# Six gate projections moved from direct to seven-product form, the heads' work dealt to three lanes, and a new tile order, in a one-core decoder block

## The chip, the core and the metric

The kernel runs on one core of a Trainium2 chip. Its engines are TensorE (PE, matmuls; PEld is its weight load), VectorE (DVE), ScalarE (ACT), GpSimd (POOL) and SyncE (SP), whose queue issues most DMAs; each works through its own queue of instructions in order. The metric is the device time of one execution in microseconds (us). Where a time is compared, it is the median of several executions.

## The reference

A decoder block on 1024 positions of width 1024 with 16 meta positions in front, one layer, all in float32:

```python
p     = h @ w_in + b_in        # columns: u_s5 | q | k | v | o | i | f | g_s5 | g_m
y_s5  = GLU(GELU(S5(u_s5)))                       # grouped complex-diagonal state-space model
y_m   = (o * HeadNorm(mLSTM(q, k, v, i, f))) @ m_w_out   # 4 heads, chunkwise
mix   = sigmoid(g_s5) * y_s5 + sigmoid(g_m) * y_m
h     = LN(alpha * h + mix @ w_o)
h     = LN(alpha * h + relu(h @ w_up + b_up)^2 @ w_down)
```

Here `o` is a sigmoid of its own projection, and q and k pass through a causal convolution of width 4 and a SiLU.

## The kernel before

Every float32 operand is split into a high and a low part (`whi`, `wlo`; `hT_hi`, `hT_lo`), and every product is made of three matmuls, high by high, low by high and high by low (`mm3`, lines 229 to 237). Features are tiled by 128, positions by up to 512. A projection tile is a **job**: it loads its weights (`wraw`), has them split by ScalarE and VectorE (`split_w`, line 208; the split of the next job is issued while this one runs), and runs 24 matmuls for each block of positions into a PSUM bank, which an engine then evacuates.

The job letters of `ORDER` (line 41) are: q0 to q3 the query and key tiles of a head, v the values, u the input of the state-space part (S5), o the output gates of the mLSTM, g the gates g_s5, m two of the gates g_m. Behind them follow the eight GLU tiles z0 to z7. A gate job has two halves of 512 positions, so 48 matmuls of 128x512.

Everything that is not a projection runs in **lanes** (line 90): generators that issue a few instructions and then yield a number, an estimated time until their next step. `pump()` (line 154), called after every two blocks of a projection, lets each lane go on whose number is used up. So the numbers at the top of the file (`ML`, `NL`, `C5`, `K5`, ...) set how the small instructions are spread among the projections; a list scheduler then fixes the order on each engine. Lane `ml` holds the four heads one behind the other. Head h (`mlstm`, line 438) makes its decay tables (`gB`, `wiB`, `qi`), then goes through nine chunks: per chunk `pk` (transpose of k) and `pS` (scores), then `pn` (read-out with the state `C`) and `pu` (the update). The normalisation `N` (line 503), once for chunks 1 to 4 and once for 5 to 8, ends in the transposes `pt` of `hraw` and two ScalarE evacuations into `hmF`.

An o job multiplies its sigmoid (`osig`) into `hmF`, and needs the head finished. The loop at line 1523 sees to that:

```python
            while int(j.tag[1:]) not in HMREADY:
                lanes["cv"].drain()
                lanes["ml"].step()
```

It issues the steps of the head at once, before the o job's own instructions.

`ah_scale` (line 1405) scales the normed input by alpha times gain and adds alpha times bias, in eight tiles `ahr` of 128x1024 that are loaded from `ah0_dr`, worked on by two VectorE instructions each and stored to `ah_dr`. It starts with o6 and shares lane `ah` with `up_early`, which prepares the first weights of the up projection.

Behind z7 `run7` works through two stages of class `Seven` (line 1024). There a pair of output tiles is computed from quarter blocks by **seven** products in place of eight, with sums of weight blocks that GpSimd's queue has made by accumulating DMAs into `ws_dr` (`w_sums`, line 973), and differences of position blocks that VectorE makes and splits in place into `hT` (`to_home`). A product is a unit of 12 matmuls of 128x512. Stage g has three pairs, the six gates g_m that are not in `ORDER`; stage y has four, the projection `m_w_out`. The units go product by product over all pairs (`SEQ7`). The output projection with its layer norm and the up and down projections follow; these too use seven products.

PSUM has eight banks: five for tag `mm`, three for tag `sd`. SBUF has a pool of 30 slots of 128x1056.

Of the kernel before, what the change touches and what calls it, by code (L numbers as in the profile page):

```python
# [14 lines left out]
P = 128  # L15
# [44 lines left out]
GY = 6.0  # L60
GS = 1.8
# [58 lines left out]
def decoder_block(  # L120
# [7 lines left out]
    big = ctx.enter_context(tc.tile_pool(name="big", bufs=30, side="left"))  # L128
# [22 lines left out]
    lanes = {"ml": Lane(), "cv": Lane(), "s5": Lane(), "s5c": Lane(), "s5g": Lane(), "ah": Lane(), "gp": Lane()}  # L151
# [136 lines left out]
    def qk_job(h, isk):  # L288
# [12 lines left out]
        def conv_steps(pre):  # L301
            y = slot("cy")
            a_.activation(y[:, :LEN], pre[:, 0:LEN], AF.Identity, scale=convt[:, ci, 0:1], bias=convt[:, ci, 4:5])
            for w in range(1, 4):
# [8 lines left out]
            QK[h, isk] = r
            yield 0.5
        fm_job(JQ + ci, BLK0 if len(all_jobs) < 4 else BLK, 0, evac, done)

    def v_job(h):
# [6 lines left out]
        def run(job):  # L324
# [41 lines left out]
            if h == 0:  # L366
                lanes["ml"].add(gates())
# [70 lines left out]
    def mlstm(h):  # L438
        while (h, 1) not in QK:
            yield 0.5  # L440
        qT, kT, vt = QK[h, 0], QK[h, 1], VT[h]
# [15 lines left out]
        yield 4.0
# [45 lines left out]
        def N(half, hm):  # L503
# [12 lines left out]
            for f in range(2):  # L516
# [70 lines left out]
    def s5_pre():  # L587
# [38 lines left out]
        es = slot("s5E")  # L626
        E = es[:, 0:288].rearrange("p (r e q) -> p r e q", r=2, q=16)
# [45 lines left out]
        bb = slot("s5bb")  # L673
        S5["bb"] = bb
# [250 lines left out]
    def glu_job(f):  # L925
        def run(job):
# [6 lines left out]
            MIX[f] = SG.pop(f)  # L933
# [16 lines left out]
            for zz in (1, 0):  # L950
                for bi, (c0, c1) in enumerate(HALF):
# [6 lines left out]
                    else:  # L958
                        v_.tensor_tensor(z2[:, c0:c1], ps, z2[:, c0:c1], op=OP.mult)
# [132 lines left out]
    def gate_evac(n, p, ps):  # L1092
        f1, f2 = NM + 2 * p, NM + 2 * p + 1
# [69 lines left out]
    def gates_and_output():  # L1163
        h00, h10, h01, h11 = home(0, 0), home(1, 0), home(0, 1), home(1, 1)
        g = Seven(3, wf, JGM + NM, 0, {1: h00, 2: h10, 6: h01, 7: h00, 4: h10, 5: h01, 3: h11})
        y = Seven(4, wmo, 0, 3, {1: h00, 2: h10, 6: h01, 7: h11, 4: h00, 5: h10, 3: h01})
# [24 lines left out]
        def hm_load():  # L1191
            for nm, kh, ch in (("11", 0, 0), ("12", 0, 1), ("22", 1, 1), ("21", 1, 0)):
                M[nm] = raw_block(hm_dr, kh, ch)

        def y_start():
            for i in range(3):
# [5 lines left out]
                  7: [lambda: to_home(M["11"], h00), lambda: now(sub(M["12"], M["12"], M["22"]))],  # L1202
# [26 lines left out]
    def ln0_pipe(xs, jobs):  # L1229
# [66 lines left out]
        def pair_banks(p):  # L1296
            tr[p] = [sdps("ln0"), sdps("ln0"), sdps("ln0"), mmps("ln0")]
# [211 lines left out]
    for i, j in enumerate(jobs):  # L1509
# [30 lines left out]
        if i >= 5 and i % 2 and ws:  # L1540
# [583 lines left out]
```

## Time and profile before

| | us |
|---|---|
| median of three executions | 1530.55 |
| lowest and highest of them | 1529.15 and 1532.7 |
| the profiled execution | 1528.6 |
| its span, first to last instruction | 1526.7 |

Times in the profile count from the span's start. The opening layer norm with the first q jobs lasts to about 75 us, the projections with all lanes to 575, the GLU tiles to 664, stage g to 715, stage y to about 790, the output projection with its layer norm to 895, and the up and down projections take the rest. The rows to read are the busy time of each engine by stretch, the waits of TensorE, and the instructions in order of time where it waits. A matmul's row lasts longer than the distance to the next one, since matmuls overlap.

### The profile page before, as it was taken

The numbers are of one execution on the slowest core, as the hardware profiler recorded it, in microseconds if no ns is written. First come the engines' busy times: TensorE is split into PE (matmuls) and PEld (weight loads), VectorE is DVE, ScalarE is ACT, GpSimd is POOL, SyncE is SP. The second block draws the span as 40 slices with busy tenths as digits, with TensorE's granted clock in tenths as the row PEclk, the third lists the DMA queues.
The fourth block names the chain that finished last, engine by engine and source line by source line (L and its number), as shares of the span: only waits on it lengthen the run. The fifth ranks groups of instructions, "written<-read, shape, count | busy, mean of one in ns | idle before, by whom it ended". The sixth has DMA issues, their size and how long they took to land.

```text
span 1526.7 us, 20426 instructions
## 1 busy us (share of the span) xinstructions
PE 1500.7 (98%) x7593; PEld 1269.9 (83%) x7593; DVE 1044.7 (68%) x1895; ACT 659.7 (43%) x1027; POOL 79.9 (5%) x183
## 2 busy tenths in 40 slices
PE   7999899999999998999999999999999999999997
PEld 7998799988998887888788888888888888888886
DVE  7785755447655558768697575766666679767786
ACT  5631644354464453345443253444444534433340
POOL 0000000022032000000000001000000000000000
PEclk9999999999999999999999999999999999999999
DMA  8504132422654369955351238544443897767652
GB/s 304 190 25 137 35 78 80 132 79 89 182 118 97 92 209 350 343 196 191 117 201 70 96 115 265 186 155 149 152 147 134 280 386 274 250 224 237 204 176 100
DMA packets 122147, 261.18 MB, mean 171 GB/s; under 512 B 14568, under 2 KB 36784, under 8 KB 122048
## 3 DMA queue, kind: packets, MB, share of 16 engines
q1 hardware_dynamic: 111344, 233.00, 44.7%
q0 software_dynamic: 10704, 26.88, 7.1%
q8 instruction: 60, 0.98, 0.3%
q14 instruction: 39, 0.32, 0.1%
HBM read 188.78 MB, written 84.55 MB: 179 GB/s over the span
## 4 chain that ended last, share of the span: by engine, by line
PE 78%; issue 16%; DMA 2%; DVE 2%; ACT 1%; SPq 0%; POOLq 0%; ACTq 0%; DVEq 0%
PE mm L235 19%; PE mm L233 19%; PE mm L234 19%; PE sd L234 4%; PE sd L233 4%; PE sd L235 4%; PE mm L1341 2%; DMA x<-in_x_dram 1%; PE pu L483 1%; PE pn L479 1%; PE pn L480 1%; DMA ahr<-ah_dr 1%; DVE ahr L1422 1%; PE pS L469 1%; PE s5z L820 0%
## 5 line engine op out<-in xcount | busy, mean ns | idle before, releaser
L233 PE MATMUL mm<-hT_hi,whi 128*128 128x512 f32 (+3 forms) x604 | 230.2, 381 | 0.0
L235 PE MATMUL mm<-hT_hi,wlo 128*128 128x512 f32 (+3 forms) x604 | 226.3, 377 | 0.1
L234 PE MATMUL mm<-hT_lo,whi 128*128 128x512 f32 (+3 forms) x604 | 225.1, 373 | 0.0
L233 PEld LDWEIGHTS mm<-hT_hi,whi 128*128 128x128 f32 x604 | 113.6, 188 | 18.7 <-issue 1.2
L235 PEld LDWEIGHTS mm<-hT_hi,wlo 128*128 128x128 f32 x604 | 113.5, 188 | 18.4 <-DVE wlo L1063 0.5
L234 PEld LDWEIGHTS mm<-hT_lo,whi 128*128 128x128 f32 x604 | 113.7, 188 | 16.5
L1819 ACT ACTIVATE dah<-da 128x1024 fp32r<-128x1024 f32 x56 | 58.6, 1052 | 89.6 <-PE sd L234 39.6
L234 PE MATMUL sd<-dwl,dah 128*128 128x512 f32 x240 | 94.5, 394 | 0.0
L233 PE MATMUL sd<-dwh,dah 128*128 128x512 f32 x240 | 94.3, 393 | 0.0
L235 PE MATMUL sd<-dwh,dal 128*128 128x512 f32 x240 | 94.1, 393 | 0.0
L1823 ACT ACTIVATE dwh<-wdr 128x1024 fp32r<-128x1024 f32 x56 | 58.9, 1053 | 80.2 <-DVE wdr L1808 19.6
L1820 DVE TENSOR_TENSOR dal<-da,dah 128x1024 fp32r<-128x1024 f32 x56 | 68.1, 1219 | 25.1 <-ACT dah L1819 24.3
L234 PE MATMUL mm<-dwl,dah 128*128 128x512 f32 (+1 forms) x224 | 84.5, 378 | 0.0
L233 PE MATMUL mm<-dwh,dah 128*128 128x512 f32 (+1 forms) x224 | 84.4, 377 | 0.0
L235 PE MATMUL mm<-dwh,dal 128*128 128x512 f32 (+1 forms) x224 | 84.4, 377 | 0.0
L1824 DVE TENSOR_TENSOR dwl<-wdr,dwh 128x1024 fp32r<-128x1024 f32 x56 | 68.2, 1219 | 11.6 <-ACT dwh L1823 11.0
L233 PE MATMUL mm<-whi,hT_hi 128*128 128x256 f32 (+1 forms) x256 | 73.9, 289 | 0.0
L234 PE MATMUL mm<-wlo,hT_hi 128*128 128x256 f32 (+1 forms) x256 | 73.1, 285 | 0.0
L235 PE MATMUL mm<-whi,hT_lo 128*128 128x256 f32 (+1 forms) x256 | 72.8, 285 | 0.0
L220 DVE TENSOR_TENSOR wlo<-wraw,whi 128x1024 fp32r<-128x1024 f32 (+1 forms) x46 | 55.9, 1220 | 21.9 <-ACT whi L219 21.1
L235 PE MATMUL mm<-th,wul 128*128 128x512 f32 x156 | 61.4, 394 | 0.0
L234 PE MATMUL mm<-tl,wuh 128*128 128x512 f32 x156 | 61.3, 393 | 0.0
(480 smaller groups left out, 3649.7 us busy)
## 6 DMA issues: line engine op xcount, KB each, us to landing
da<-act_dr SPq DMA_DIRECT2D x56, 512.0 KB, 5.9
wdr<-in_wdn_dram SPq DMA_DIRECT2D x56, 512.0 KB, 6.0
wur<-in_wup_dram SPq DMA_DIRECT2D x32, 512.0 KB, 4.3
act_dr<-upy SPq DMA_DIRECT2D x64, 256.0 KB, 2.5
wraw<-in_wf_dram SPq DMA_DIRECT2D x30, 512.0 KB, 3.6
wu_dr<-wpre SPq DMA_DIRECT2D x21, 512.0 KB, 6.5
wpre<-wu_dr POOLq DMA_DIRECT2D x21, 512.0 KB, 4.9
act_dr<-upx SPq DMA_DIRECT2D x32, 256.0 KB, 3.8
```

What stands on the lines that cost most here:

```text
L220: todo.append(lambda e=v_, r=r, hi=hi, lo=lo, n=n: e.tensor_tensor(lo[:, :n], r[:, :n], f32(hi[:, :n]), op=OP.subtract))
L233: t_.matmul(ps, ah, bh, start=(i == 0 and part[0]), stop=False, skip_group_check=skip)
L234: t_.matmul(ps, ah, bl, start=False, stop=False, skip_group_check=skip)
L235: t_.matmul(ps, al, bh, start=False, stop=(i == n - 1 and part[1]), skip_group_check=skip)
L469: t_.matmul(ps[:, :P], kT[:, c0:c0 + n], qT[:, c0:c0 + n], start=True, stop=True)
L479: t_.matmul(pn[:, :257], qi[:, c0:c0 + n], Cs[c][:, :257], start=True, stop=False)
L480: t_.matmul(pn[:, :257], sws[c], vt[c][:, :257], start=False, stop=True)
L1341: t_.matmul(acc[w][:, :c1 - c0], jobs[i].w[0][a][:, k * P:(k + 1) * P], (hT_hi, hT_lo)[b][:, k, c0:c1], start=(first and k == 0), stop=(la ...
L1819: a_.activation(ah[:, :D], a[:, :D], AF.Copy)
L1820: v_.tensor_tensor(alo[:, :D], a[:, :D], f32(ah[:, :D]), op=OP.subtract)
L1823: a_.activation(wh, raw[i], AF.Copy)
L1824: v_.tensor_tensor(wl, raw[i], f32(wh), op=OP.subtract)
```

## The change

- The gates g4 to g7 of g_s5 (`GP` = 2 pairs) and all eight gates g_m (4 pairs) are made by stage g of `run7`, six pairs instead of three. The direct jobs m0, m1, g4 to g7 go. A z job from z4 on writes its product without the gate, and `mix_gate_evac` multiplies the gate in later.
- The units of `Seven` go by `CHAINS` and by groups of pairs: products 1 and 2 of the first group, then of the second, then 6, 7, 4, then 5, 3. `w_sums` makes sums for ten pairs and sends them more often from job 20.
- The heads have three lanes: `mp` (gates and decay tables, `prepare`), `ml` (chunks) and `mn` (normalisation). The loop ahead of an o job steps all three. `qi` takes the place of `wiB`, and q and k stay in the convolution's tile `cy`.
- `ORDER` is new; S5 starts at u0; all yield numbers are new.
- `ah_scale` starts with `run7`.
- PSUM has four banks of each tag; the opening layer norm, the b chain of stage y and the x banks of the down projection take `sd`. The pool has 31 slots.

```diff
-ORDER = "q0 q1 v0 v1 g0 o1 q2 v2 q3 o3 u0 u1 o0 m0 u2 g5 o2 o4 o5 u3 v3 m1 g7 g6 g2 g4 g1 g3 o6 o7"
-S5_START = "v1"
-NM = 2
+WS2 = 20
+ORDER = "q0 q1 v0 u0 v1 u1 q2 g0 v2 o0 o1 u2 q3 v3 u3 o2 o3 g1 o4 o5 g2 g3 o6 o7"
+S5_START = "u0"
+GP = 2
+SF = 8 - 2 * GP
-ML = [2.87, 1.8, 1.8, 2.49]
-NL = [4, 1.69, 1.5, 2.01]
+ML = [1.8, 1.8, 1.8, 1.8]
+CY = 1.8
+PB = 8.5
+PG = 0.3
+PE = 4.0
+NL = [1.6, 1.6, 1.6, 1.6]
...
-AH_START = "o6"
-AHY = 1.2
+AH_START = "run7"
+AHY = 3.6
...
-    big = ctx.enter_context(tc.tile_pool(name="big", bufs=30, side="left"))
+    big = ctx.enter_context(tc.tile_pool(name="big", bufs=31, side="left"))
...
-        return psum.tile([P, 512], F32, tag="mm", bufs=5, name=name)
+        return psum.tile([P, 512], F32, tag="mm", bufs=4, name=name)
...
-        return psum.tile([P, 512], F32, tag="sd", bufs=3, name=name)
+        return psum.tile([P, 512], F32, tag="sd", bufs=4, name=name)
...
             if c == 5:
-                yield from N(0, nrm[0])
-        yield 1.5
-        yield from N(1, nrm[1])
-        HMREADY.update((2 * h, 2 * h + 1))
+                lanes["mn"].add(N(0, nrm[0]))
+        lanes["mn"].add(N(1, nrm[1]))
...
-            MIX[f] = SG.pop(f)
+            MIX[f] = SG.pop(f) if f in SG else slot("mix")
...
+                        if f >= SF:
+                            v_.tensor_tensor(MIX[f][:, c0:c1], ps, z2[:, c0:c1], op=OP.mult)
+                            continue
...
-    SEQ7 = (1, 2, 6, 7, 4, 5, 3)
-    ws_dr = dram.tile([7, 4, P, 512], F32, name="ws_dr")
+    CHAINS = ((1, 2), (6, 7, 4), (5, 3))
+    ws_dr = dram.tile([GP + 8, 4, P, 512], F32, name="ws_dr")
...
-            self.units = [(n, p) for n in SEQ7 for p in range(npair)]
+            at = [range(sum(groups[:i]), sum(groups[:i + 1])) for i in range(len(groups))]
+            self.units = [(n, p) for ch in CHAINS for ps in at for n in ch for p in ps]
...
+        def gate(x, src, b, f, half):
+            a_.activation(x, src, AF.Sigmoid, bias=b)
+            m = MIX[f][:, 512 * half:512 * half + 512]
+            v_.tensor_tensor(m, x, m, op=OP.mult)
...
-        g = Seven(3, wf, JGM + NM, 0, {1: h00, 2: h10, 6: h01, 7: h00, 4: h10, 5: h01, 3: h11})
-        y = Seven(4, wmo, 0, 3, {1: h00, 2: h10, 6: h01, 7: h11, 4: h00, 5: h10, 3: h01})
+        g = Seven((GP, 4), wf, JGS + SF, 0, {1: h00, 2: h10, 6: h01, 7: h00, 4: h10, 5: h01, 3: h11})
+        y = Seven((4,), wmo, 0, GP + 4, {1: h00, 2: h10, 6: h01, 7: h11, 4: h00, 5: h10, 3: h01})
...
             while int(j.tag[1:]) not in HMREADY:
                 lanes["cv"].drain()
-                lanes["ml"].step()
+                for n in ("mp", "ml", "mn"):
+                    lanes[n].step()
...
     first()
+    if AH_START == "run7":
+        lanes["ah"].add(ah_scale())
     run7()
+    lanes["ah"].drain()
```

The order of the instructions moves at three places of which the prediction speaks. The first is TensorE at head 0's last chunks. Before, two chunks and the first transposes stand in a row:

```order
L479 MATMUL pn<-C,qi 128x257
L480 MATMUL pn<-v_882,sw 128x257
L483 MATMUL pu<-v_882,kw 128x257
L464 MATMUL pk<-ident,kT 128x128
L469 MATMUL pS<-qT,kT 128x128
L479 MATMUL pn<-C,qi 128x257
L480 MATMUL pn<-v_883,sw 128x257
L483 MATMUL pu<-v_883,kw 128x257
L521 MATMUL pt<-ident,hraw 128x128 x2
L464 MATMUL pk<-ident,kT 128x128
L521 MATMUL pt<-ident,hraw 128x128 x4
L469 MATMUL pS<-qT,kT 128x128
```

Now, at a chunk of the same head (pk and pS read the convolution's tile `cy`, and `wiB` holds what was `qi`):

```order
L496 MATMUL pn<-C,wiB 128x257
L497 MATMUL pn<-v_882,sw 128x257
L500 MATMUL pu<-v_882,kw 128x257
L240 MATMUL mm<-hT_lo,whi 128x400
L241 MATMUL mm<-hT_hi,wlo 128x400
L481 MATMUL pk<-ident,cy 128x128
L486 MATMUL pS<-cy 128x128
L239 MATMUL mm<-hT_hi,whi 128x400
```

Matmuls of a query or key job now stand between the steps of a chunk.

The second place is the change from z0 to z1, where `z2s` is the evacuation of a bank of a z job and `whi_5804` (before) or `whi_5397` (now) is the high half of z1's weights. ScalarE before:

```order
L522 ACTIVATE hmF_5441<-pt_5573,mngt_87 128x512
L522 ACTIVATE hmF_5454<-pt_5579,mngt_87 128x512
L955 ACTIVATE z2s_5749<-mm_5750 128x512
L955 ACTIVATE z2s_5749<-mm_5764 128x512
L219 ACTIVATE whi_5804<-wraw_5663 128x1024
L955 ACTIVATE z2s_5830<-mm_5831 128x512
```

ScalarE now:

```order
L920 ACTIVATE osig_5319<-mm_5322,bft_83 128x512
L972 ACTIVATE z2s_5352<-mm_5353 128x512
L225 ACTIVATE whi_5397<-wraw_5286 128x1024
L972 ACTIVATE z2s_5352<-mm_5363 128x512
L972 ACTIVATE z2s_5421<-mm_5422 128x512
```

The high half has moved ahead of the second evacuation. On VectorE the low half stood, before, among rows of `ah_scale`:

```order
L959 TENSOR_TENSOR z2s_5749<-mm_5775,z2s_5749 128x512
L959 TENSOR_TENSOR z2s_5749<-mm_5789,z2s_5749 128x512
L960 TENSOR_TENSOR sgs_1698<-z2s_5749,sgs_1698 128x512
L1422 TENSOR_TENSOR ahr_5734<-ahr_5734,gB0_5596 128x1024
L220 TENSOR_TENSOR wlo_5805<-wraw_5663,whi_5804 128x1024
L960 TENSOR_TENSOR sgs_1698<-z2s_5749,sgs_1698 128x512
L1422 TENSOR_TENSOR ahr_5734<-ahr_5734,bB0_5597 128x1024
```

On VectorE now:

```order
L921 TENSOR_TENSOR hmF_5052<-hmF_5052,osig_5319 128x512 x2
L979 TENSOR_TENSOR z2s_5352<-mm_5373,z2s_5352 128x512
L226 TENSOR_TENSOR wlo_5398<-wraw_5286,whi_5397 128x1024
L980 TENSOR_TENSOR sgs_2360<-z2s_5352,sgs_2360 128x512
L979 TENSOR_TENSOR z2s_5352<-mm_5383,z2s_5352 128x512
```

No row of `ah_scale` is left there.

The third place is ScalarE at the first GELU tile of S5 (`gelf`, and its high half `gelh`). Before, it stands behind copies of the S5 lanes:

```order
L775 ACTIVATE s5RS_4382<-s5Ri_4091 64x512 x2
L889 ACT_TABLE_LOAD
L889 ACTIVATE gelf_4449<-s5yc_4207 128x8x128
L892 ACTIVATE gelh_4451<-gelf_4449 128x1024
L876 ACTIVATE s5Y_4443<-s5y_4444 128x512
```

Now it stands between head 1's first normalisation and the sigmoids of o1:

```order
L539 ACTIVATE hmF_3175<-pt_3176,mngt_87 128x512
L539 ACTIVATE hmF_3193<-pt_3194,mngt_87 128x512
L906 ACT_TABLE_LOAD
L906 ACTIVATE gelf_3200<-s5yc_2981 128x8x128
L514 ACTIVATE hraw_3054<-pn_3216 128x257
L909 ACTIVATE gelh_3202<-gelf_3200 128x1024
L920 ACT_TABLE_LOAD
L920 ACTIVATE osig_3206<-mm_3129,bft_83 128x512
L920 ACTIVATE osig_3206<-mm_3209,bft_83 128x512
```

The GELU, its split and a table load have come between the evacuation of head 1's transposes and the release of two mm banks.

More of the change, by code (lines that the diff above doesn't have):

```diff
@@ L366, in run @@
             if h == 0:
-                lanes["ml"].add(gates())
+                lanes["mp"].add(gates())
+            lanes["mp"].add(prepare(h))
             lanes["ml"].add(mlstm(h))
@@ L436, in bcast_row, with prepare @@
                                   ap=[[0, P], [4 * P, NCH - 1], [1, P]]))
-    def mlstm(h):
-        while (h, 1) not in QK:
+    PREP, ACTIVE = {}, {}
+    def prepare(h):
+        while (h, 1) not in QK or h - ACTIVE.get("head", -1) > 1:
             yield 0.5
-        qT, kT, vt = QK[h, 0], QK[h, 1], VT[h]
+        qT = QK[h, 0]
         gB, wiB = slot("gB"), slot("wiB")
@@ L451, in mlstm @@
                                     mask[:n, :n], op0=OP.subtract, op1=OP.max)
-            yield 0.3
+            yield PG
         a_.activation(gB[:META, 0:META], gB[:META, 0:META], AF.Exp, scale=-1.0)
         a_.activation(gB[:, META:LEN], gB[:, META:LEN], AF.Exp, scale=-1.0)
+        v_.tensor_copy(dec[:, 0:9], wiB[:, META - 1:LEN:P])
+        qi = wiB
         v_.tensor_tensor(qi[:, META:LEN], qT[:, META:LEN], wiB[:, META:LEN], op=OP.mult)
-        v_.tensor_copy(dec[:, 0:9], wiB[:, META - 1:LEN:P])
-        yield 4.0
+        yield PE
+        PREP[h] = (gB, qi, dec)
+    def mlstm(h):
+        while h not in PREP:
+            yield 0.5
+        ACTIVE["head"] = h
+        gB, qi, dec = PREP.pop(h)
+        qT, kT, vt = QK[h, 0], QK[h, 1], VT[h]
         kws, sws, Cs = {}, {}, {}
@@ L524, in N @@
                 yield 1.2
+            if half:
+                HMREADY.update((2 * h, 2 * h + 1))
         A(0)
@@ L1115, in gate_evac, with mix_gate_evac @@
             a_.activation(c12, c12, AF.Sigmoid, bias=b1)
+    GT = {}
+    def mix_gate_evac(n, p, ps):
+        f1, f2 = SF + 2 * p, SF + 2 * p + 1
+        b1, b2 = (bft[:, JGS + f:JGS + f + 1] for f in (f1, f2))
+        if n == 1:
+            if p % 2 == 0:
+                GT["p", p // 2] = slot("gtp")
+            GT["u", p] = slot("gtu")
+        if n in (1, 6, 7, 4):
+            p1 = GT["p", p // 2][:, p % 2 * 512:p % 2 * 512 + 512]
+        u2, u3 = GT["u", p][:, 0:512], GT["u", p][:, 512:1024]
+        def gate(x, src, b, f, half):
+            a_.activation(x, src, AF.Sigmoid, bias=b)
+            m = MIX[f][:, 512 * half:512 * half + 512]
+            v_.tensor_tensor(m, x, m, op=OP.mult)
+        if n == 1:
+            a_.activation(p1, ps, AF.Copy)
+        elif n == 2:
+            gate(u2, ps, b1, f1, 0)
+        elif n == 6:
+            v_.tensor_tensor(u2, ps, p1, op=OP.subtract)
+        elif n == 7:
+            v_.tensor_tensor(u3, ps, p1, op=OP.subtract)
+        elif n == 4:
+            v_.tensor_tensor(p1, ps, p1, op=OP.subtract)
+            gate(p1, p1, b2, f2, 0)
+            if p % 2 == 1 or p == GP - 1:
+                GT.pop(("p", p // 2))
+        elif n == 5:
+            v_.tensor_tensor(u3, ps, u3, op=OP.add)
+            gate(u3, u3, b2, f2, 1)
+        else:
+            v_.scalar_tensor_tensor(u2, ps, -1.0, u2, op0=OP.mult, op1=OP.subtract)
+            gate(u2, u2, b1, f1, 1)
+            GT.pop(("u", p))
     YT = {}
@@ L1191, in hm_load, with hm_last @@
         def hm_load():
-            for nm, kh, ch in (("11", 0, 0), ("12", 0, 1), ("22", 1, 1), ("21", 1, 0)):
+            for nm, kh, ch in (("11", 0, 0), ("12", 0, 1), ("22", 1, 1)):
                 M[nm] = raw_block(hm_dr, kh, ch)
+        def hm_last():
+            M["21"] = raw_block(hm_dr, 1, 0)
         def y_start():
@@ L1215, in run @@
             g.run(lambda c, p: sdps() if c == "b" else mmps(), gate_evac, ghooks)
-            y.run(lambda c, p: sdps() if c == "b" and p else mmps(), ym_evac, yhooks)
+            y.run(lambda c, p: sdps() if c == "b" else mmps(), ym_evac, yhooks)
         return token_sums, early, begin, first, run
```

53 lines of the change are left out of this document (27 added, 26 removed).

## The prediction

> **What bounds the kernel now.** I read the page's busy times and chain first, then the busy time by stretches, then TensorE's waits, and last the two places where it waited, in order of time.
>
> ```profile
> PE 1500.7 (98%) x7593; PEld 1269.9 (83%) x7593; DVE 1044.7 (68%) x1895; ACT 659.7 (43%) x1027; POOL 79.9 (5%) x183
> PE 78%; issue 16%; DMA 2%; DVE 2%; ACT 1%; SPq 0%; POOLq 0%; ACTq 0%; DVEq 0%
> ```
>
> TensorE is busy for 98% of the span and carries most of the chain that ended last. So the time is the work of TensorE plus the few places in which it stands, and an edit counts only if it takes products away, or makes or ends a wait of TensorE.
>
> ```profile
> core 0: us, PE busy (x) PEld busy (x) DVE busy (x) ACT busy (x) POOL busy (x), PEclk, DMA share, GB/s
> 75.00:575.00 500.00, 495.35 (x2954) 442.62 (x2953) 299.24 (x729) 228.25 (x376) 62.91 (x140) 1.00 0.38 105
> 170.00:575.00 405.00, 405.00 (x2351) 361.11 (x2350) 235.49 (x528) 196.98 (x330) 58.11 (x115) 1.00 0.41 113
> 575.00:600.00 25.00, 21.13 (x90) 16.57 (x90) 23.09 (x28) 5.55 (x8) 1.45 (x2) 1.00 1.00 327
> 664.00:715.00 51.00, 51.00 (x222) 41.19 (x221) 39.70 (x41) 28.91 (x34) 0.00 (x0) 1.00 0.53 181
> 735.00:895.00 160.00, 160.00 (x721) 130.43 (x720) 125.53 (x274) 58.10 (x146) 2.20 (x4) 1.00 0.34 116
> ```
>
> The direct projections run from 75 to 575. From 170 on, TensorE has no idle time at all; what is missing lies before 170, and again at 575 to 600. The seven-product gate stage (664 to 715) and the output stages behind it are full.
>
> ```profile
> engine line waited for: us in total, times, longest us
> PE pt L521 <- DVE hraw L514: 3.1, 1, 3.1
> PE mm L233 <- ACT whi L219: 2.5, 1, 2.5
> PE pS L469 <- ACT kw L466: 1.6, 3, 0.5
> PE mm L235 <- DVE wlo L220: 1.4, 1, 1.4
> ```
>
> These are six waits outside the opening layer norm (whose code stays): 4.7 us at head 0's chunks, 3.9 us at z1.
>
> **Fewer products.** A direct gate job is 8 blocks of K, three products and two halves, 48 matmuls of 128x512. A pair of the seven-product stage is 7 x 4 x 3 = 84 and stands for two jobs. Six direct jobs go (288 matmuls) and three pairs come (252): 36 fewer.
>
> ```profile
> 574.82 0.40 PE L234 MATMUL mm<-gell,whi 128*128 128x512 f32 x1
> ...
> 580.58 0.40 PE L235 MATMUL mm<-gelh,wlo 128*128 128x512 f32 x1
> 583.43 0.50 PE L233 MATMUL mm<-gelh,whi 128*128 128x512 f32 x1 [2.45 <-ACT whi L219]
> ...
> 585.17 0.40 PE L234 MATMUL mm<-gell,whi 128*128 128x512 f32 x1
> 586.98 0.50 PE L235 MATMUL mm<-gelh,wlo 128*128 128x512 f32 x1 [1.42 <-DVE wlo L220]
> ```
>
> From the first to the second of these rows lie 25 steps in 5.76 us, 0.2304 us each (the 0.40 of a row overlaps the next). 36 x 0.2304 = **8.3 us less**. The direct stage loses 288 x 0.2304 = 66.4 us and the gate stage gains 58.1.
>
> The Trainium skill ("TensorE: Matmul & The Clock Gate", section Back-to-back issue gap) gives N/2.4 + 2.5 ns for an isolated matmul and about 131 ns sustained at N = 512. By the first the term would be 36 x 0.2158 = 7.8 us, by the second 4.7 us. The trace is slower than both, and its spacing decides.
>
> **Head 0's waits.** The loop ahead of an o job steps lane ml until the head is normalised. With o1 in sixth place it pours head 0's last chunks out while only o1's own matmuls are there to fill.
>
> ```profile
> 155.09 0.49 PE L469 MATMUL pS<-qT,kT 128*128 128x128 f32 x2 [0.52 <-ACT kw L466]
> ...
> 157.51 0.49 PE L469 MATMUL pS<-qT,kT 128*128 128x128 f32 x2 [0.52 <-ACT kw L466]
> ...
> 161.12 0.60 PE L483 MATMUL pu<-v,kw 128*128 128x257 f32 x2
> 164.82 0.44 PE L521 MATMUL pt<-ident,hraw 128*128 128x128 f32 x2 [3.10 <-DVE hraw L514]
> ```
>
> A bare chunk has 0.52 us of waiting, and the normalisation 3.10. In the order of the changed kernel every chunk of head 0 has projections between its steps, and the first o job stands tenth; so I take all 4.7 us as gone. The wait of 3.10 has a second price:
>
> ```profile
> 160.00:165.00 5.00, 1.90 (x10) 1.39 (x11) 3.61 (x18) 1.97 (x3) 0.00 (x0) 1.00 0.00 0
> 165.00:170.00 5.00, 5.00 (x23) 4.22 (x23) 1.74 (x7) 3.42 (x6) 0.00 (x0) 0.66 0.32 102
> ```
>
> Behind it the granted clock is 0.66 over 5 us: 0.34 x 5 = 1.7 us more. Behind the waits of 2.45 and 1.42 us it stays at 1.00.
>
> **z1's waits.** These rows of ScalarE and VectorE stand ahead of them:
>
> ```profile
> 580.78 1.09 ACT L955 ACTIVATE z2s<-mm 128x512 f32<-128x512 f32 x2 [5.87 <-PE mm L234]
> 582.32 1.06 ACT L219 ACTIVATE whi<-wraw 128x1024 fp32r<-128x1024 f32 x1 [0.45 <-DMA hm_dr<-hmF]
> ...
> 584.57 1.22 DVE L1422 TENSOR_TENSOR ahr<-ahr,gB 128x1024 f32<-128x1024 f32 x1
> 585.71 1.22 DVE L220 TENSOR_TENSOR wlo<-wraw,whi 128x1024 fp32r<-128x1024 f32 x1
> ```
>
> Before, z1's high half stands on ScalarE behind both evacuations of z0's first two banks, which start only as z0 ends, and its low half on VectorE among ah_scale's rows. Now whi follows the first evacuation (nine matmuls, 2.1 us, before z0 ends, against 0.55 and 1.06 us of ScalarE), and ah_scale is out of VectorE's queue. 3.9 us go; what is late next is that whi itself, by 0.3 us at most.
>
> Each of the six waits is longer than its row says, since a matmul's row is 0.40 and the pitch 0.23: 6 x 0.17 = 1.0. Together 4.7 + 1.7 + 3.9 + 1.0 = **11.3 us less**.
>
> **New waits.** Three places in the changed order give little cover. First, ahead of o0 stand eight transposes of head 0, eight for the S5 tables, pk and pS with no projection between: two waits of the kind of pS, 1.0 us. Second, ScalarE at head 1's first normalisation:
>
> ```profile
> 560.23 2.35 ACT L889 ACTIVATE gelf<-s5yc 128x1024 f32<-128x1024 f32 x1 [0.90 <-PE pn L479]
> 562.36 0.43 ACT L497 ACTIVATE hraw<-pn 128x257 f32<-128x257 f32 x1
> 562.70 1.04 ACT L892 ACTIVATE gelh<-gelf 128x1024 fp32r<-128x1024 f32 x1
> ...
> 568.46 1.28 ACT L903 ACT_TABLE_LOAD   x1
> 569.75 1.27 ACT L903 ACTIVATE osig<-mm,bft 128x512 f32<-128x512 f32 x2
> 573.65 1.27 ACT L522 ACTIVATE hmF<-pt,mngt 128x512 f32<-128x512 f32 x2 [2.63 <-PE pt L521]
> ```
>
> Between the last transpose and the release of o1's first bank now stand both hmF, a table load, gelf, hraw, gelh, a table load and one osig: 1.27 + 1.28 + 2.35 + 0.43 + 1.04 + 1.28 + 0.64 = 8.3 us. With four mm banks instead of five, TensorE reaches a product that wants that bank after about 6.6 us of other rows: 1.7 us. Third, z1's 0.3. Sum **3 us more**. No row shows these places; the bounds are 0 (405 us from 170 on went without idle) and 8 (each of the three at the longest wait seen, 3.1, less what overlaps).
>
> **What I cost at nothing.** ah_scale's 16 rows go to the gate stage, which will last 42 units x 12 x 0.2304 = 116 us.
>
> ```profile
> L1422 DVE TENSOR_TENSOR ahr<-ahr,gB x8: 1217/1218/1226, 558.6 to 590.7; 128x1024 f32<-128x1024 f32 x8
> DMA to landing us min/median/max: 2.6/4.0/10.6
> L1063 DVE TENSOR_TENSOR wlo<-wraw,whi 128x1024 fp32r<-128x1024 f32 x9 | 11.0, 1221 | 6.2 <-ACT whi L1062 6.1
> L1104 DVE TENSOR_TENSOR sgm<-sd,sgm 128x512 f32<-128x512 f32 x3 | 2.1, 684 | 0.0
> ```
>
> VectorE then has 21 splits, 14 home splits, 8 differences and 16 rows of ah_scale at 1.22 us, and 38 evacuations at 0.685: 72 + 26 = 98 of 116 us, 84% after 78% (39.70 of 51.00). That fits, with 18 us to spare. The transfers ah_scale takes along (16 of 512 KB) leave a stretch with DMA share 1.00 for one with 0.53. The three further pairs of weight sums go through GpSimd's queue, whose engine is busy for 5% of the span. The lanes' VectorE work (299 us less ah_scale's 20) meets 433 us instead of 500: 65% instead of 60%. The bank split (4 and 4) keeps four banks for each opening pair; in the later stages a unit of 2.8 us stands against evacuations of 0.7. If the cover of ah_scale fails, that is the second rival.
>
> **Sum.** The profiled execution took 1528.6 us (span 1526.7, 1.9 outside). 1528.6 - 8.3 - 11.3 + 3 = 1512.0. The median of the runs shown is 1530.55, 2.0 above that execution; on its scale **1514**.
>
> **Rivals.**
> 1. The waits only move. Fewer filler jobs are left (four direct gates, not ten), and what head 0 saves comes back at other heads. Only the 8.3 us stay: 1520.3, on the median's scale 1522. For it: the lanes' chains are as long as before. Against: 65% of VectorE, and chunks spaced by projections in the order.
> 2. VectorE binds the gate stage. Its rows run in order, so a split behind a late ahr waits too, as the 1.42 at z1 did. If four of the eight tiles land at 10.6 instead of 4.0, that is 26 us, 8 beyond the 18 to spare: 1522. Against: two tiles are loaded ahead.
> 3. Slower: the filler runs out at the heads' ends. Each head is normalised twice; a bare one costs 3.3 us and 1.7 of low clock, 5.0. All eight: 1514 + 40 = 1554; four give 1534, where slower begins. Against: from 170 to 575 the kernel before has six such places and no wait; for it: 66 us of filler less.
>
> On the clock, the Trainium skill ("TensorE: Matmul & The Clock Gate", section What's actually happening) says that a window of about 3.4 us without work halves the array's clock until a busy window has passed; 3.4 us at half rate are 1.7 us, and the 0.66 behind the 3.1 us wait agrees. By this rule rival 3 pays twice, while shorter waits pay once.
>
> **How the numbers follow.** Forecast (1506 to 1518) 0.54; rival 1 0.20; rival 2 0.08; no new waits and more saved (below 1506) 0.06; rival 3 0.12, of which two waits or so (1525 to 1527.5) 0.03, about four (within 0.2%, which is what a measurement of this kernel can tell from no change, 3.1 us) 0.05, more 0.04. Range 1505 to 1525: up to rivals 1 and 2, about 0.84. Faster 0.91, same 0.05, slower 0.04.
>
> **What would show it.** The waits pt on hraw and pS on kw gone and no slice with a clock below 1 after 100 us; z1 starting right behind z0; 4824 matmuls of 128x512; the gate stage 116 us long with TensorE full and VectorE near 84%. It is wrong if TensorE waits for ahr's neighbours (wlo, whi) there, or idles at the ends of heads 1 to 3 for more than 8 us in all.

## The result, and the profile after

| | us |
|---|---|
| changed kernel, median of 4 executions | 1540.6 (1538.64 to 1542.21) |
| kernel before in the same comparison | 1531.32 (1529.15 to 1532.7) |
| ratio | 1.0058, 95% interval 1.0044 to 1.0071 |
| profiled execution of the changed kernel, and its span | 1540.15, 1538.4 |
| profiled execution of the kernel before | 1528.6 |

The change made the kernel slower by 0.58%. The forecast was 1514 us, with 4 in 100 for slower. The profiled executions differ by 11.6 us. The page of the changed kernel, busy times and chain:

```profile
PE 1501.7 (98%) x7557; PEld 1270.8 (83%) x7557; DVE 1057.3 (69%) x1914; ACT 661.7 (43%) x1033; POOL 86.9 (6%) x183
PE 65%; issue 17%; DMA 8%; DVE 5%; ACT 3%; SPq 1%; POOLq 0%; DVEq 0%; ACTq 0%
```

TensorE has 36 matmuls fewer (7557 after 7593), as counted. But its share of the chain that ended last fell from 78% to 65%; DMA, VectorE and ScalarE took what it lost. The busy time by stretch, in the columns of before: from 75 to 575 us, as before; the direct stage from 170 to 520; the GLU tiles; and most of stage g, which lasts from 611 to 734 us.

```profile
75.00:575.00 500.00, 483.02 (x2868) 432.25 (x2867) 309.91 (x759) 227.77 (x386) 69.01 (x136) 0.98 0.47 131
170.00:520.00 350.00, 338.46 (x1985) 300.83 (x1984) 218.51 (x537) 177.81 (x310) 60.82 (x114) 0.98 0.48 124
520.00:612.00 92.00, 92.00 (x401) 74.84 (x400) 55.29 (x73) 30.07 (x48) 0.00 (x0) 1.00 0.72 266
612.00:730.00 118.00, 114.18 (x483) 90.81 (x482) 86.43 (x92) 50.88 (x60) 0.00 (x0) 0.99 0.58 199
```

From 75 to 575 us TensorE now idles for 17.0 us (4.7 before). The GLU tiles, where z1 waited, are full. The waits of TensorE of 1 us and more, without the opening layer norm's:

```profile
PE s5z L837 <- DVE sw L488: 4.7, 1, 4.7
PE sd L239 <- DVE sgm L1127: 3.0, 1, 3.0
PE pt L538 <- DVE hraw L531: 2.4, 1, 2.4
PE mm L239 <- DVE v L366: 2.3, 1, 2.3
PE mm L239 <- DVE mlo L360: 2.2, 1, 2.2
PE mm L239 <- ACT osig L920: 1.8, 1, 1.8
PE s5k L783 <- DVE C L503: 1.2, 1, 1.2
PE pn L496 <- DVE C L503: 1.0, 1, 1.0
PE s5p L776 <- ACT kw L483: 1.0, 1, 1.0
```

With four below 1 us (0.6, 0.5, 0.3 and 0.2) these are 21.2 us in thirteen places. VectorE is named in most. Behind the six longest, from 1.8 us up, the granted clock falls; two of the stretches of 5 us behind a wait:

```profile
85.00:90.00 5.00, 4.09 (x21) 4.09 (x22) 4.37 (x9) 0.88 (x1) 0.00 (x0) 0.66 0.01 3
272.00:277.00 5.00, 3.97 (x12) 3.29 (x13) 4.76 (x19) 1.28 (x5) 0.00 (x0) 0.50 0.14 50
```

At 0.66 that is 1.7 us lost, as at the one such place of before. Over 10-us stretches from 75 to 1515 us, the clock's shortfall is 1.7 us before and 11.9 us now (one minus the clock, times 10, summed).

The balance of the profiled executions: products -8.3, old waits -8.6 (4.7 and 3.9), new waits +21.2, clock +10.2, the opening layer norm's waits -1.6 (8.3 to 6.7): +12.9, against 11.6 measured.

How a wait comes about is seen on VectorE, in order of time, ahead of the longest one (s5z, at 268):

```profile
262.67 0.48 DVE L505 SCALAR_TENSOR_TENSOR C<-C,dec,pu 128x257 f32<-128x257 f32 x1
263.06 0.21 DVE L515 TENSOR_SCALAR dd<-pn,ecol 128x1 f32<-128x1 f32 x1
263.19 0.42 DVE L517 BATCH_NORM_STATS2 hst<-pn 128x6 f32<-128x256 f32 x1
271.08 0.17 DVE L463 COPY dec<-wiB 128x9 f32<-128x9 f32 x1 [7.46 <-DMA s5yc<-ys_dr]
271.48 0.18 DVE L518 BATCH_NORM_AGGREGATE hmv<-hst 128x2 f32<-128x6 f32 x1 [0.23 <-DVE dec L463]
271.58 1.19 DVE L465 TENSOR_TENSOR wiB<-cy,wiB 128x1024 f32<-128x1024 f32 x1
272.69 0.28 DVE L488 TENSOR_TENSOR sw<-pS,gB 128x128 f32<-128x128 f32 x1
```

VectorE stands for 7.46 us at `dec`, the first reader of head 2's `wiB`, whose load, issued at 255.5 us and 15.5 us long, lands at 271.0 us (the row names another load on the same queue). Behind it in the queue stands head 1's `sw`, which frees the PSUM bank that the S5 product s5z wants. The view of the tile gB has how long VectorE stood idle for its loads (us, times):

```profile
  DMA gB<-grow_dr: 18.1, 5
```

And the view of the tile wiB how long its loads took:

```profile
DMA to landing us min/median/max: 7.0/10.4/15.5
```

VectorE stood 18.1 us for gB (5.4 before), and wiB's loads took 7.0 to 15.5 us (5.1 to 10.1 before).

### The profile page after: what moved, and what is told of

Same layout as the page of the kernel before. It is cut to its first block, busy times and chain, and to the rows that moved or that the text cites. A ratio compares the mean times of both kernels' runs of the same rounds, so it can differ in the third digit from the quotient of the medians.

```text
span 1538.4 us, 20329 instructions
## 1 busy us (share of the span) xinstructions
PE 1501.7 (98%) x7557; PEld 1270.8 (83%) x7557; DVE 1057.3 (69%) x1914; ACT 661.7 (43%) x1033; POOL 86.9 (6%) x183
## 4 chain that ended last, share of the span: by engine, by line
PE 65%; issue 17%; DMA 8%; DVE 5%; ACT 3%; SPq 1%; POOLq 0%; DVEq 0%; ACTq 0%
PE mm L239 16%; PE mm L241 16%; PE mm L240 16%; PE sd L241 3%; PE sd L240 3%; PE sd L239 3%; PE mm L1405 1%; DMA wdr<-in_wdn_dram 1%; DMA gB<-grow_dr 1%; DMA x<-in_x_dram 1%; DMA wiB<-wrow_dr 1%; PE pn L496 1%; PE pn L497 1%; PE pu L500 1%; DMA arow<-res_dr 1%
## 5 line engine op out<-in xcount | busy, mean ns | idle before, releaser
L239 PE MATMUL mm<-hT_hi,whi 128*128 128x512 f32 (+3 forms) x544 | 207.3, 381 | 4.3 <-DVE v L366 2.3
L240 PE MATMUL mm<-hT_lo,whi 128*128 128x512 f32 (+3 forms) x544 | 203.8, 375 | 0.0
L241 PE MATMUL mm<-hT_hi,wlo 128*128 128x512 f32 (+3 forms) x544 | 201.7, 375 | 0.6 <-DVE wlo L1084 0.6
L240 PE MATMUL sd<-dwl,dah 128*128 128x512 f32 x320 | 125.7, 393 | 0.0
L241 PE MATMUL sd<-dwh,dal 128*128 128x512 f32 x320 | 125.4, 392 | 0.0
L239 PE MATMUL sd<-dwh,dah 128*128 128x512 f32 x320 | 121.9, 393 | 0.0
L240 PEld LDWEIGHTS mm<-hT_lo,whi 128*128 128x128 f32 x544 | 103.5, 190 | 14.6 <-issue 0.2
L1888 DVE TENSOR_TENSOR dal<-da,dah 128x1024 fp32r<-128x1024 f32 x56 | 68.2, 1219 | 25.5 <-issue 11.6
L239 PEld LDWEIGHTS sd<-dwh,dah 128*128 128x128 f32 x320 | 60.1, 188 | 14.0
L241 PEld LDWEIGHTS sd<-dwh,dal 128*128 128x128 f32 x320 | 60.0, 188 | 13.8
L240 PEld LDWEIGHTS sd<-dwl,dah 128*128 128x128 f32 x320 | 60.1, 188 | 13.5
```

What stands on the lines that cost most here:

```text
L239: t_.matmul(ps, ah, bh, start=(i == 0 and part[0]), stop=False, skip_group_check=skip)
L240: t_.matmul(ps, ah, bl, start=False, stop=False, skip_group_check=skip)
L241: t_.matmul(ps, al, bh, start=False, stop=(i == n - 1 and part[1]), skip_group_check=skip)
L1888: v_.tensor_tensor(alo[:, :D], a[:, :D], f32(ah[:, :D]), op=OP.subtract)
```

## The experiments

Two theories stood against each other. A: the new lanes put instructions that wait for a load ahead of another head's steps, the tables above all. B, later F: the projections taken out were the filler of the direct stage, and waits come back wherever one is cured. Medians in us; each ratio is to the kernel before, run beside it.

| run | median | ratio (95% interval) |
|---|---|---|
| tables_in_chunk_lane | 1535.22 | 1.0034 (1.0024 to 1.0045) |
| tables_later | 1541.18 | 1.0067 (1.0049 to 1.0086) |
| banks_5_3 | 1554.85 | 1.0156 (1.0136 to 1.0176) |
| ah_scale_at_o6 | 1540.19 | 1.0051 (1.0032 to 1.0069) |
| products_only | 1573.79 | 1.0281 (1.0260 to 1.0302) |
| products_o1_later | 1578.03 | 1.0304 (1.0284 to 1.0323) |
| products_ah_in_run7 | 1566.06 | 1.0232 (1.0216 to 1.0249) |
| sub_later | 1539.07 | 1.0052 (1.0037 to 1.0067) |
| two_gates_back | 1544.12 | 1.0090 (1.0074 to 1.0106) |
| four_gates_back | 1528.33 | 0.9978 (0.9966 to 0.9990) |
| two_gates_back_tables_ah | 1535.93 | 1.0034 (1.0021 to 1.0046) |
| tables_lane_conv_pace | 1529.63 | 0.9989 (0.9978 to 0.9999) |
| ah_pace | 1533.27 | 1.0021 (1.0011 to 1.0031) |
| four_gates_back_pace | 1531.04 | 1.0001 (0.9992 to 1.0010) |
| four_gates_back_all | 1532.19 | 1.0017 (1.0005 to 1.0028) |
| before_o1_later | 1533.15 | 1.0015 (1.0005 to 1.0025) |
| before_ah_in_run7 | 1538.69 | 1.0051 (1.0039 to 1.0064) |
| before_both | 1539.37 | 1.0056 (1.0044 to 1.0069) |

### The products alone

The kernel before, with only the parts of the diff that touch GP, CHAINS, w_sums, Seven, the z jobs and the gate evacuations:

```diff
-ORDER = "q0 q1 v0 v1 g0 o1 q2 v2 q3 o3 u0 u1 o0 m0 u2 g5 o2 o4 o5 u3 v3 m1 g7 g6 g2 g4 g1 g3 o6 o7"
+ORDER = "q0 q1 v0 v1 g0 o1 q2 v2 q3 o3 u0 u1 o0 u2 o2 o4 o5 u3 v3 g2 g1 g3 o6 o7"
```

> The kernel before with the seven-product part of the change alone: six direct gate jobs out of the old order, gate stage with six pairs, CHAINS, w_sums and mix_gate_evac as changed; the lanes, all yield numbers, ah_scale at o6, five and three banks stay as before. Theory A (the loss is made by the new lanes, numbers and bank split, the 36 products are worth their 8.3 us): 1520 to 1526, with head 0's waits at 154 to 165 us and z1's in place. Theory B (the six direct jobs were needed as filler): 1529 or more, with new waits between 170 us and z0.

It took 1573.79 us. Its longest waits of TensorE:

```profile
PE s5y L875 <- DVE s5w L863: 11.2, 1, 11.2
PE mm L235 <- ACT gelh L894: 9.2, 2, 8.5
PE pt L523 <- DVE hraw L516: 6.5, 3, 3.1
PE mm L235 <- ACT whi L221: 6.4, 2, 6.1
PE s5z L822 <- DMA s5U<-us_dr: 5.7, 1, 5.7
```

And its busy time from the end of the direct stage on:

```profile
520.00:600.00 80.00, 52.99 (x239) 43.69 (x238) 53.63 (x79) 29.82 (x50) 0.00 (x0) 0.81 0.67 215
```

The direct jobs end some 70 us sooner, at 497 us instead of 568, but the S5 lanes do not: their last product stands at 550 (536 before). What is left of their chain (scan, read-out, GELU, split) runs bare, with 27 of 80 us idle and a clock of 0.81. That is theory B's range, and by far: 8.3 us of products were bought with some 50 us. Part of it may belong to the old order and its yield numbers, with which S5 starts late; no run separates that from the cover. In the changed kernel, where S5 starts at u0, its last product stands at 485 us, ahead of the first GLU tile at 522. So this tail is not what the changed kernel pays for; its new lanes, order and numbers together win back 33 of the 50.

With o1 moved as well (`... v1 g0 q2 v2 o1 q3 ...`):

> The kernel of products_only with o1 moved in the order from behind g0 to behind v2. Head 0's chunks then stand among the projections q2 and v2. Theory A: the waits at 154 to 165 us and the low clock behind them go: 6 us less than products_only, if no other place takes them over; 1514 to 1521. Theory B (the time that head 0 saves comes back at later heads): within 2 us of products_only.

It took 1578.03 us, 4.2 more than products_only: not faster, as theory B says, but outside the 2 us that it allowed.

### Filler back into the changed kernel

```diff
-ORDER = "q0 q1 v0 u0 v1 u1 q2 g0 v2 o0 o1 u2 q3 v3 u3 o2 o3 g1 o4 o5 g2 g3 o6 o7"
-GP = 2
+ORDER = "q0 q1 v0 u0 v1 u1 q2 g0 v2 o0 o1 g4 u2 q3 v3 g5 u3 o2 o3 g1 g6 o4 o5 g2 g7 g3 o6 o7"
+GP = 0
```

> The changed kernel with GP 0: g4 to g7 are direct jobs again, spread over the order (g4 behind o1, g5 behind v3, g6 behind g1, g7 behind g2), 24 matmuls more in all (5.5 us), stage g with four pairs and without its first group. Theory F: the waits from 250 to 430 us nearly go, 1526 to 1536. Rival L: 1544 or more.

1528.33, 12.3 us below the changed kernel although it has 24 matmuls more, 5.5 us: the range of theory F. The stretch from 75 to 575 us:

```profile
75.00:575.00 500.00, 492.70 (x2933) 439.30 (x2932) 295.81 (x736) 224.38 (x378) 68.18 (x136) 0.99 0.40 108
```

TensorE idles for 7.3 us there instead of 17.0, and the clock's shortfall is 3.4 instead of 10.2. The profiled executions lie 11.7 us apart: 16.5 us come from this stretch (9.7 of idle time and 6.8 of clock) and 3.6 from stage g (1.9 and 1.7), less 5.5 for the products and 1.0 for the opening layer norm, 13.6 by this sum. Of all runs it is the fastest, and faster than the kernel before by 0.22% (0.10 to 0.34%).

Two gates back (GP 1; g4 behind o1, g5 behind u3):

> The changed kernel with GP 1: two gates (g4 behind o1, g5 behind u3) are direct jobs again, 96 matmuls more in the direct stage, 84 fewer in the gate stage, 12 more in all (2.8 us). Theory F (filler: the direct stage has too few projections to cover the chains of heads and S5, each wait also costing clock): the waits and the low clock from 250 to 430 us (some 19 us) fall by more than the 2.8 us, 1530 to 1538. Rival L (the lanes' order alone makes the waits): they stay, 1541 to 1545.

1544.12: outside the range of theory F and inside that of rival L. In the direct stage the waits on osig and pt went and that on v fell to 0.3 us, but a new one of 4.1 us (pS on C) came, and stage g waited 7.8 us (whi 3.0 and 1.6, sgm 2.5, gtp 0.7) instead of 3.8. The middle between two orders is not the middle of their times.

### The tables' lane

```diff
-                lanes["mp"].add(gates())
-            lanes["mp"].add(prepare(h))
+                lanes["ml"].add(gates())
+            lanes["ml"].add(prepare(h))
```

> The changed kernel with the tables of each head (prepare, and the gates) back in lane ml, so that no head's tables are made while another head's chunks run; the normalisation keeps its own lane. Theory A: the new waits come from VectorE and ScalarE standing in their queues for a table load (gB, wiB) with steps of another head or job behind them. Then the waits s5z on sw (4.7 us at 268) and pt on hraw (2.4 at 387) go, with the low clock behind them, and the time falls by 8 to 16 us from 1540.6. Theory B: the waits come from too few projections as filler and from four mm banks. Then they come back elsewhere and the time stays within 4 us of 1540.6.

1535.22, 5.4 us less: between the two ranges. The wait of s5z went, and those of pt became four:

```profile
PE pt L538 <- DVE hraw L531: 4.9, 4, 2.2
```

That the tables stand in another head's way is shown for this wait; it is a part of the loss, not the whole.

> The changed kernel with PB 20 in place of 8.5: the lane waits longer between the issue of a head's table loads and the first instruction that reads them. Theory A: the idle time of VectorE until gB and wiB (18.1 and 0.8 us, and 7.5 put down to s5yc) falls below 6 us, at least two of the waits at 142, 268 and 387 us go, and the time falls by 8 to 16 us from 1540.6. Theory B: the time stays within 4 us, since the loads only set which row waits.

The edit (`PB = 20.0`) did not do what it was to test: VectorE still stood 17.7 us for gB, now in seven places. The time, 1541.18, says nothing on theory A.

### The banks

```diff
-        return psum.tile([P, 512], F32, tag="mm", bufs=4, name=name)
+        return psum.tile([P, 512], F32, tag="mm", bufs=5, name=name)
...
-        return psum.tile([P, 512], F32, tag="sd", bufs=4, name=name)
+        return psum.tile([P, 512], F32, tag="sd", bufs=3, name=name)
```

> The changed kernel with five mm banks and three sd banks as before (and with the bank lists of the opening layer norm, stage y and the down projection as before; the first b chain of the gate stage's second group on mm). Theory A: only the two waits of a projection for a bank go (mlo at 83, 2.2 us, and osig at 298, 1.8 us), 4 to 6 us with the clock behind the first, and the sd waits (s5z, s5p, s5k) grow a little: 1534 to 1540. Theory B: the banks are the main cause and the time falls by 10 us or more.

1554.85. The waits on mlo at 83 us, on v at 142 and on osig at 298 went, so these come from four mm banks. But with three sd banks one late table (VectorE stands 10.7 us for gB at 154) stops everything:

```profile
PE pS L486 <- DVE sw L488: 13.2, 1, 13.2
PE s5k L783 <- issue: 5.6, 1, 5.6
```

The new lanes need four sd banks; neither theory had the time rise.

### ah_scale and stage g

VectorE of the changed kernel ahead of the wait on sgm, at 679 us:

```profile
674.39 0.69 DVE L1127 TENSOR_TENSOR sgm<-sd,sgm 128x512 f32<-128x512 f32 x1
679.72 1.23 DVE L1037 TENSOR_TENSOR rawb<-rawb 128x1024 f32<-128x1024 f32 x1 [4.64 <-DMA rawb<-hm_dr]
...
682.00 0.69 DVE L1127 TENSOR_TENSOR sgm<-sd,sgm 128x512 f32<-128x512 f32 x1
```

The evacuation stands behind a difference whose load of hm is late, and these loads are issued on SyncE's queue among ah_scale's stores, which wait for VectorE.

```diff
-AH_START = "run7"
-AHY = 3.6
+AH_START = "o6"
+AHY = 1.2
```

> The changed kernel with ah_scale started at job o6 with its old pace, not in the gate stage. Theory A: the wait of 3.0 us on sgm at 679 and the low clock behind it go (4.8 us); z1 may wait again (3.9 us before): 1535 to 1541. A theory that ah_scale is the main cause of the loss asks for 1530 or less.

1540.19: the wait on sgm went, a wait of 2.2 us with low clock came back at the GLU tiles. As theory A had it, an exchange.

```diff
-                  7: [hm_last, lambda: to_home(M["11"], h00), lambda: now(sub(M["12"], M["12"], M["22"]))],
-                  4: [lambda: to_home(M["21"], h10), lambda: now(sub(M["11"], M["11"], M["12"]))],
+                  7: [hm_last, lambda: to_home(M["11"], h00)],
+                  4: [lambda: to_home(M["21"], h10), lambda: now(sub(M["12"], M["12"], M["22"])),
+                      lambda: now(sub(M["11"], M["11"], M["12"]))],
```

> The changed kernel with one VectorE difference of the gate stage (M12 - M22) moved from hook 7 to hook 4, two instructions. Theory A: the wait of 3.0 us on sgm at 679 stood behind that difference, which waited 4.6 us for its load of hm; it goes with its low clock, 3 to 5 us less than 1540.6. Rival: the wait on the loads only passes to the next VectorE instruction (hT_lo of the same loads) and the time stays within 2 us.

1539.07, and the wait stayed at 3.2 us. But the order on VectorE, which the list scheduler fixes, did not change; a difference still stands ahead of the split and the evacuation:

```profile
678.54 1.23 DVE L1037 TENSOR_TENSOR rawb<-rawb 128x1024 f32<-128x1024 f32 x1 [4.75 <-DMA rawb<-hm_dr]
679.68 1.22 DVE L1033 TENSOR_TENSOR hT_lo<-rawb,hT_hi 128x1024 fp32r<-128x1024 f32 x1
680.82 0.68 DVE L1127 TENSOR_TENSOR sgm<-sd,sgm 128x512 f32<-128x512 f32 x1
```

So the edit did not do what it was to test, and the run decides nothing between theory A and the rival.

```diff
-AHY = 3.6
+AHY = 2.4
```

> The changed kernel with ah_scale's pace alone changed, 2.4 in place of 3.6. If the wait on sgm at 679 us comes from hm's loads standing behind ah_scale's stores on SyncE's queue, it goes with its low clock: 1534 to 1537 instead of 1540.6, with the direct stage as it was. If VectorE's work in the stage is the cause, a faster pace makes it worse: 1541 or more.

1533.27, 7.3 us less by the medians, 5.7 by the ratios, a little more than forecast: ah_scale is through before hm is loaded, the loads are issued 7.7 us earlier (660.2 instead of 667.9 us; 2.8 of it because the stage starts earlier), and the wait is gone. So the wait came from the queue, not from VectorE's load. Not all of the gain is the wait's. The profiled executions differ by 6.6 us; the wait and the clock behind it are 4.7 of them. Another 3.4 are clock in the direct stage, which the edit doesn't touch: its waits have nearly the same lengths as in the changed kernel, but behind those at 298 and 387 us the clock stayed at 1.00 this time.

On products_only, ah_scale in stage g with the edit of sub_later:

> The kernel of products_only with ah_scale started with the gate stage at the changed pace (3.6), and the difference M12 - M22 of hook 7 moved behind hook 4. Theory A: z1's two waits (3.9 us) go and no wait on sgm comes: 3 to 5 us less than products_only. Rival: VectorE or the queue of SyncE binds in the gate stage, which then has waits of 4 us or more; same as or slower than products_only.

1566.06, 7.7 us below products_only: the direction of theory A, but not its path. z1 waited only 0.9 us in products_only (0.2 now). What went is the wait of 5.7 us of s5z on its load of us_dr, and the one on z0's first split fell from 6.1 to 4.1 us.

### Combinations

tables_lane_conv_pace is tables_in_chunk_lane with `AHY = 2.4` and `CY = 1.2`. The other three join such settings with filler: the tables' lane and `AHY = 2.4` on two_gates_back; `AHY = 2.4` alone on four_gates_back; and on that the tables' lane and `CY = 1.2`.

> tables_in_chunk_lane with the convolutions at their old pace (CY 1.2) and ah_scale at pace 2.4. If the wait on mlo at 84 us (2.2 us and 1.7 of clock) comes from convolution instructions that stand ahead of the evacuation on VectorE because of the slower pace, it goes, and the time falls by 3 to 5 us from 1535.2; if it comes from four mm banks alone, it stays. The wait on sgm (3.7 us) goes with the faster ah_scale, or stays if hm's loads are late for another reason.

> two_gates_back with the tables in lane ml (as in tables_in_chunk_lane) and ah_scale at pace 2.4 in place of 3.6. Theory F with A: the gains of both add up in part, 1524 to 1533; a wait on sgm in the gate stage goes if the loads of hm no longer stand behind ah_scale's stores on SyncE's queue.

> four_gates_back with ah_scale's pace 2.4. Its gate stage has one wait of 1.6 us on whi; with the faster pace it goes or stays: 1525 to 1529. A stage of four pairs is shorter (78 us), so if the pace overloads VectorE there, 1531 or more.

> four_gates_back_pace with the tables in lane ml and CY 1.2. If the filler and the tables' lane are separate causes they add up: the waits pn on C at 159 and s5z on sw at 265 go, 1519 to 1525. If the filler already covers what the tables' waits cost, it stays within 3 us of four_gates_back_pace.

tables_lane_conv_pace took 1529.63 us, 5.6 less than tables_in_chunk_lane: no wait on sgm; the wait at 84 us stayed (2.4 us), as banks_5_3 says. Its stretch from 75 to 575 us:

```profile
75.00:575.00 500.00, 489.23 (x2914) 434.89 (x2913) 318.30 (x771) 237.77 (x397) 63.22 (x136) 1.00 0.49 137
```

TensorE idles for 10.8 us instead of 17.0, and the clock's shortfall to 1515 us is 1.7 instead of 11.9 (in the quickest of its executions, which is the profiled one). No gate was put back here. So 11 of the 12.3 us that the filler gives come without filler too, by three settings of the lanes; it is 0.11% faster than the kernel before (0.01 to 0.22%), so about as fast.

Put together with filler, the gains did not add up: 1535.93, 1531.04 and 1532.19. The first is 8.2 us below two_gates_back but outside its range, the second 2.7 above four_gates_back, the third within the 3 us that stand for "the filler already covers it". Each order had its own waits, among them one of 6.6 us on hraw (two_gates_back_tables_ah) and one of 2.9 us on a split in stage g (four_gates_back_pace).

### The forecast waits, one by one, in the kernel before

All runs above that touch the old waits take filler out as well. The next three leave every job of the kernel before in place:

```diff
-ORDER = "q0 q1 v0 v1 g0 o1 q2 v2 q3 o3 u0 u1 o0 m0 u2 g5 o2 o4 o5 u3 v3 m1 g7 g6 g2 g4 g1 g3 o6 o7"
+ORDER = "q0 q1 v0 v1 g0 q2 v2 o1 q3 o3 u0 u1 o0 m0 u2 g5 o2 o4 o5 u3 v3 m1 g7 g6 g2 g4 g1 g3 o6 o7"
```

> The kernel before with o1 moved from behind g0 to behind v2, all jobs direct as before. If head 0's waits are a local matter, 6 us go (4.7 of waits, 1.7 of clock): 1523 to 1527. If they only move to another head, within 3 us of 1531.

1533.15. Two waits of TensorE, from its instructions in order of time:

```profile
253.90 0.49 PE L469 MATMUL pS<-qT,kT 128*128 128x128 f32 x2 [0.52 <-ACT kw L466]
258.79 0.69 PE L521 MATMUL pt<-ident,hraw 128*128 128x128 f32 x2 [3.10 <-DVE hraw L514]
```

Nothing waits at 154 to 165 any more; one wait of each kind, of the same length, now stands at head 1, at 253 to 259, ahead of o3, with the same 1.7 us of clock behind it. Two of the three waits on kw are gone, but a new one of 1.3 us (pk on C) came at 321, and z1's grew from 3.9 to 4.3.

```diff
-AH_START = "o6"
-AHY = 1.2
+AH_START = "run7"
+AHY = 4.8
...
     first()
+    lanes["ah"].add(ah_scale())
     run7()
+    lanes["ah"].drain()
```

> The kernel before with ah_scale started with the gate stage, at a pace of 4.8, so that it spreads over stages g and y. z1's two waits (3.9 us) go: 1526 to 1529. If it binds VectorE or SyncE's queue in stage g of three pairs, 1531 or more.

1538.69. z1 runs through, and stages g and y wait instead, on the splits of their weights:

```profile
PE mm L235 <- DVE wlo L1063: 6.5, 3, 3.9
```

With those on whi they are 8 us, and the clock falls to 0.93 from 664 to 740 us, another 5 us. The pace of 4.8 is the only one tried here.

> The kernel before with both edits. If the two add up: 1518 to 1524, faster than both kernels; if one of them only moves its wait, 1525 to 1530.

1539.37, above both ranges: nothing adds up, and the two costs stand side by side.

## Why the prediction was wrong

- **Fewer products: right.** 36 matmuls fewer; stage g took 123 us (forecast 116), 3.8 of them idle and 1.7 lost to the clock. VectorE was busy for 74% of it, not 84%. (In the kernel before, stage g's 252 matmuls last to about 721 us; the 715 given for it is too early.)
- **Head 0's and z1's waits: right that they go, wrong that this is a gain.** None of the six is in the list after. But before_o1_later shows head 0's wait as the place where a chain comes to light, not a mistake at that place: cured there, it comes out at the next head. z1's, cured in before_ah_in_run7 at pace 4.8, is paid for in the next stage; in ah_pace, with six pairs and pace 2.4, neither z1 nor stage g waits for more than 0.5 us at a time, so that part could be had. The 11.3 us were counted as if each wait were its own cause.
- **New waits, "3 us more" with bounds of 0 and 8: the step that failed.** They were 21.2 us and, with the clock's further 10.2 us, 31.4. The named places came at their size: osig 1.8 (forecast 1.7), pS ahead of o0 0.5 (1.0), z1 none (0.3). Missing were the others: s5z 4.7, sgm 3.0, pt 2.4, v 2.3, mlo 2.2. The lower bound rested on 405 us without idle in the kernel before; but there the six jobs that go were part of the cover, and products_only shows that without them the old lanes stand bare for 27 of 80 us. Why the new lanes wait is shown for five of the places: mlo, v and osig for want of a fifth mm bank (banks_5_3), s5z for a table that stands ahead of another head's step (tables_in_chunk_lane), sgm for hm's late loads (ah_pace). For pt and the smaller ones it isn't.
- **"65% instead of 60%" of VectorE: the wrong measure.** The share itself came out near (63% from 75 to 522 us), but the average load of an engine says nothing on where its queue stands at a load. VectorE was not too busy; it waited, 18.1 us for gB alone.
- **"The bank split keeps four banks": wrong.** That held for the opening layer norm; behind it the v jobs use mm alone, and lost 4.5 us with their fifth bank (mlo and v).
- **ah_scale at nothing: wrong by 4.7 us** (3.0 of wait on sgm and 1.7 of clock, both gone in ah_pace), through a queue I had not followed. I counted VectorE's load in stage g (98 of 116 us) and left out that its stores stand on SyncE's queue ahead of hm's loads. The second rival named the right stage and engine, not the path.
- **The third rival was the nearest in kind:** new waits all along the heads, the longer ones paid twice. They came as thirteen of 0.2 to 4.7 us instead of eight equal ones at the heads' ends, and I gave it 0.12. That missing filler is their cause is not shown: filler takes away 12.3 us, but tables_lane_conv_pace takes away 11 without it.
- **The clock: 1.7 us for a wait that trips it, as measured before.** Seven such losses are the 11.9 us, two of them behind s5z. But the forecast had only waits like the 3.1 us pay twice; here waits of 1.8 to 2.4 us did too.

What stays open: whether the lost filler or the new lanes' settings should be called the cause, since mending either one brings the time back to that of the kernel before (four_gates_back, tables_lane_conv_pace), mending both brings no more, and no run comes near 1514. Most runs that move a lane's number or the order move many waits at once, so the causes are not separated further.

## What to carry to other kernels

On a kernel whose main engine is 98% busy, products taken out of a stage are worth their time only if that stage is bound by them; first find the longest chain that the stage covers (here S5's, whose last product stood at 536 us before, at 550 with the projections ending 70 us sooner, and at 485 once it was started earlier) and compare it with what is left. A wait that stands alone may be the outlet of such a chain: before counting it as a gain, say what is late next, and test it by moving it. Before an instruction is moved into another stage, follow every queue it uses, the DMA issue queue included.

## What the runs showed of the hardware

A wait of about 2 us can cost clock, and the same wait need not cost it each time. Behind the 2.2 us at 83 us the granted clock was 0.66 over 5 us, while behind 2.45 us at 581 us in the kernel before it stayed at 1.00. Behind the wait of 1.8 us on osig at 298 us it fell in the changed kernel's execution (first row) and did not in ah_pace's (second row), where that wait is as long:

```profile
300.00:310.00 10.00, 10.00 (x56) 9.60 (x57) 4.70 (x17) 6.95 (x11) 1.87 (x2) 0.83 0.62 210
300.00:310.00 10.00, 9.37 (x64) 9.24 (x65) 5.72 (x20) 7.57 (x12) 1.86 (x2) 1.00 0.59 209
```

So a stall of 1.8 to 2.5 us costs its own length, or 1.7 us more. The Trainium skill ("TensorE: Matmul & The Clock Gate", section What's actually happening) ties the half clock to a window of about 3.4 us without work that runs freely; that it follows a shorter wait is what these runs show beyond that. The loads of a row of wiB to all partitions took 7.0 to 15.5 us in the changed kernel and 5.1 to 10.1 before, for the same bytes.
